# Four small tiles move from behind the tile sets to ahead of them in SBUF

## The chip, the cores and the metric

The kernel runs on one core of a Trainium2 chip. Its time is device microseconds of one execution. TensorE (PE in the profile) multiplies, VectorE (DVE) and ScalarE (ACT) do arithmetic on tiles, GpSimd (POOL) does some of it too, SyncE (SP) issues the DMAs. Tiles live in SBUF, 128 partitions each with its own run of bytes; matmuls write to PSUM. A matmul has a stationary operand, loaded first by a weight load (PEld), and a moving operand that streams through column by column.

## The reference

Two encoder layers over 512 tokens of width 1024 in float32, each a mixer and an MLP, then a last RMSNorm. Layer 0 mixes with dilated window attention (16 heads in three groups of window and dilation), layer 1 with differential attention (8 heads, two maps each), both with a relative bias table.

```
for i in range(2):
    hn  = rms_norm(h, norm_mix_g[i])
    mix = dilated_window_attention(hn, ...) if i == 0 else differential_attention(hn, ...)
    h   = h + mix
    u   = relu(rms_norm(h, norm_mlp_g[i]) @ w_in[i])      # 1024 -> 4096
    h   = h + (u * u) @ w_out[i]                          # 4096 -> 1024
out = rms_norm(h, norm_final_g)
```

## The kernel before

**Data.** Activations lie transposed: the residual h is eight tiles `h0` to `h7` of 128 features by 512 tokens. Every float32 operand of a large product is split in two parts that TensorE multiplies in its fast format: a rounded tile (`Ah`, `Bh`, `Ch`, `whi`) and the remainder (`Al`, `Bl`, `Cl`, `wlo`). `mm3` (line 168) makes one product of three matmuls, lines 169 to 171: rounded by rounded, the weights' rounded part by the remainder, the weights' remainder by the rounded part. A "product" below is one of these matmuls.

**Tile sets.** Set A (eight `Ah`, eight `Al`, from `xset("A")`) holds the input of the current stage: h times the norm's gain, written by `Norm.feed` (lines 232 and 233). Set B holds hidden tiles of the MLP in even chunks, and in attention the split queries of layer 0, the keys of layer 1 and the head outputs (`oh`, `ol`), all under the tags `Bh0` to `Bl7`. Set C, in a pool of the MLP alone, holds the hidden tiles of odd chunks. Layer 0's and layer 1's attention keep their own tiles in the memory that C has later or had before.

**Stages.** `linear_steps` takes a unit of weights, 8 tiles of 128 rows by 256 columns, and for each of its two column tiles sums 8 tiles of the moving set in one PSUM bank: 24 products for a column tile, 48 for a unit, weights stationary, 512 tokens moving. The MLP runs `m_in` (moving: set A) and `m_out` (moving: B or C) in four chunks in the order in 0, in 1, out 0, in 2, out 1, in 3, out 2, out 3; each chunk is four units, 192 products. Hidden chunks 0 and 2 lie in B, 1 and 3 in C. In `values1` (line 739) and in `m_end` (line 660, the last chunk of layer 1) the roles are turned: the set's tile is stationary, 128 tokens of it, and the weights move, 256 columns.

**Weights.** `fetch` (line 140) loads a unit of 1 MB by one DMA into `raw`, ScalarE rounds it to `whi` (line 158) and VectorE makes `wlo` (line 159), two buffers each, one unit ahead.

**The norm.** `Norm.rstd` (line 252) sums squares on TensorE, VectorE scales them to `ms` (line 257), GpSimd raises them to -1/2 into `rstd` (line 259). Both are tiles of 128 partitions by 4 float32. `Norm.rows` (line 261) turns `rstd` into a row for every partition by matmuls with the identity and keeps it in `rB` (and scaled in `rBs`). This happens four times, as hooks among the first products of a stage.

**Layout.** Pools lie one behind the other in the order in which they are opened (lines 87 to 91): `const`, `hpool` (h, A, B), `rpool` (`ms`, `rstd`, `rB` two buffers each, `rBs` one), `wpool` (`raw`, `whi`, `wlo`, two buffers of 8192 bytes a partition each), `spool` (`nacc` one, `nsq` two). Behind them come the pools that open and close with a stage: for the MLP two tiles `u`, then the tiles of C. A tile of 512 float32 takes 2048 bytes a partition. A tile of 4 float32 takes 32, as sizes are rounded up to a multiple of 32.

**Order.** The tile framework plans the instructions of each engine from their dependencies, a model of times and the order in the program, and places the semaphores. It knows a buffer by its tag and the count of its buffers.

Of the kernel before, what the change touches and what calls it, by code (L numbers as in the profile page):

```python
# [11 lines left out]
F32 = mybir.dt.float32  # L12
# [7 lines left out]
P = 128  # L20
# [4 lines left out]
NB = SEQ // P  # L25
# [56 lines left out]
def tile_encoder(ctx: ExitStack, tc: tile.TileContext, x, rel_bias, gains, norm_final_g,  # L82
# [4 lines left out]
    const = ctx.enter_context(tc.tile_pool(name="const", bufs=1))  # L87
    hpool = ctx.enter_context(tc.tile_pool(name="hpool", bufs=1))
    rpool = ctx.enter_context(tc.tile_pool(name="rpool", bufs=2))
# [14 lines left out]
    def t_tile():  # L104
        return ps_t.tile([P, 512], F32, tag="t", name="t_ps")
# [114 lines left out]
    class Norm:  # L220
# [31 lines left out]
        def rstd(self):  # L252
            ps = t_tile()
            for t in range(NB):
                nc.tensor.matmul(ps[:, t:t + 1], self.acc[:, t * P:(t + 1) * P], ones, start=True, stop=True)
            ms = rpool.tile([P, NB], F32, tag="ms", name="ms")
            nc.vector.tensor_scalar(ms, ps[:, 0:NB], 1.0 / DM, EPS, op0=ALU.mult, op1=ALU.add)
            self.r = rpool.tile([P, NB], F32, tag="rstd", name="rstd")
            nc.gpsimd.tensor_tensor(self.r, ms, mhalf[:, 0:NB], op=ALU.pow)

        def rows(self, scaled=None):
# [685 lines left out]
```

## Time and profile before

| | |
|---|---|
| median of three runs | 1250.77 us (1249.84 to 1252.31) |
| profiled execution | 1250.46 us, span 1248.7 us |
| mean granted TensorE clock | 0.993 of full speed |
| PE busy | 98% of the span, 6096 matmuls |
| DVE, ACT, POOL busy | 51%, 40%, 9% |
| DMA | 115.73 MB, 93 GB/s in the mean |

A duration of a matmul in the profile is a latency: matmuls are pipelined, and one begins before the one ahead of it has ended. The pace is the time from start to start; it is read from a stretch whose first and last start are known, divided by the count in it. A share of busy time is a mean over stages.

### The profile page before, as it was taken

The page shows a single profiled execution, that of the slowest core. Times are in us where ns is not written, and L with a number is a line of the kernel's source. Part 1 is how long each engine was busy: PE and PEld are TensorE (multiplying, and loading weights), DVE is VectorE, ACT ScalarE, POOL GpSimd, SP SyncE. Part 2 cuts the span into 40 slices and gives each one's busy share as a digit, 9 for nine tenths or more (in the row PEclk, how much of TensorE's full clock was granted, in tenths as well). Part 3 has the DMA queues.
Part 4 walks back from the last instruction along what each step waited for, and adds up shares of the span by engine and source line. Part 5 has one row for each costly group of instructions (what it writes and reads, how often), then busy time and mean ns, then how long its engine had stood idle before and what let it go on. Part 6 is the DMA issues. An engine that isn't in the chain of part 4 may idle for free.

```text
span 1248.7 us, 15250 instructions
## 1 busy us (share of the span) xinstructions
PE 1223.2 (98%) x6096; PEld 1019.1 (82%) x6096; DVE 637.8 (51%) x1039; ACT 499.5 (40%) x905; POOL 116.9 (9%) x219
## 2 busy tenths in 40 slices
PE   7989999999999999999999999998999999999997
PEld 5778878788888888888888998987888888888897
DVE  7764455644433434434568677664744334344323
ACT  5452333533422323312357666653534223123133
POOL 5000000200000000000101222312300000000011
PEclk9999999999999999999999999998999999999999
DMA  7261222233223333223422343121333223332211
GB/s 228 67 136 39 68 68 68 68 101 102 97 76 98 101 101 101 75 95 102 145 75 91 98 124 101 65 82 51 101 102 102 85 85 101 101 101 97 75 65 69
DMA packets 108307, 115.73 MB, mean 93 GB/s; under 512 B 4507, under 2 KB 101915, under 8 KB 108187
## 3 DMA queue, kind: packets, MB, share of 16 engines
q1 hardware_dynamic: 108236, 114.75, 29.4%
q8 instruction: 48, 0.79, 0.3%
q14 instruction: 23, 0.19, 0.0%
HBM read 112.50 MB, written 2.24 MB: 92 GB/s over the span
## 4 chain that ended last, share of the span: by engine, by line
PE 95%; DMA 2%; DVE 1%; ACT 1%; POOL 0%; issue 0%; SPq 0%; POOLq 0%; DVEq 0%; ACTq 0%
PE acc L169 15%; PE acc L171 15%; PE acc L170 15%; PE s_ps L170 13%; PE s_ps L171 13%; PE s_ps L169 13%; PE o_ps L800 2%; PE s_ps L345 1%; PE s_ps L346 1%; PE t_ps L791 1%; DMA B<-fd 1%; PE o_ps L525 1%; PE s_ps L494 1%; PE o_ps L529 1%; PE t_ps L485 0%; DMA h<-in_x_dram 0%
## 5 line engine op out<-in xcount | busy, mean ns | idle before, releaser
L158 ACT CAST whi<-raw 128x1024 fp32r<-128x1024 f32 (+1 forms) x194 | 192.6, 1039 | 406.2 <-PE s_ps L170 223.9
L159 DVE TENSOR_TENSOR wlo<-raw,whi 128x1024 fp32r<-128x1024 f32 (+1 forms) x194 | 233.7, 1241 | 23.2 <-ACT whi L158 22.6
L169 PE MATMUL acc<-Ah,whi 128*128 128x512 f32 x472 | 187.8, 398 | 0.0
L171 PE MATMUL acc<-Ah,wlo 128*128 128x512 f32 x472 | 187.7, 398 | 0.0
L170 PE MATMUL acc<-Al,whi 128*128 128x512 f32 x472 | 187.7, 398 | 0.0
L169 PE MATMUL s_ps<-Ah,whi 128*128 128x512 f32 x360 | 143.0, 398 | 6.0 <-ACT whi L158 6.0
L170 PE MATMUL s_ps<-Al,whi 128*128 128x512 f32 x360 | 143.7, 399 | 2.5 <-DVE Al L233 2.4
L171 PE MATMUL s_ps<-Ah,wlo 128*128 128x512 f32 x360 | 142.9, 397 | 0.0
L169 PEld LDWEIGHTS acc<-Ah,whi 128*128 128x128 f32 x472 | 89.0, 188 | 20.6 <-ACT sp L338 0.5
L171 PEld LDWEIGHTS acc<-Ah,wlo 128*128 128x128 f32 x472 | 88.8, 188 | 20.7 <-DVE wlo L159 0.5
L170 PEld LDWEIGHTS acc<-Al,whi 128*128 128x128 f32 x472 | 89.0, 188 | 20.2 <-issue 0.5
L169 PEld LDWEIGHTS s_ps<-Ah,whi 128*128 128x128 f32 x360 | 68.2, 190 | 22.0 <-ACT whi L158 6.0
L170 PEld LDWEIGHTS s_ps<-Al,whi 128*128 128x128 f32 x360 | 68.2, 189 | 20.5 <-DVE Al L233 4.6
L171 PEld LDWEIGHTS s_ps<-Ah,wlo 128*128 128x128 f32 x360 | 68.2, 190 | 16.1 <-DVE wlo L159 0.2
L644 ACT ACTIVATE u<-u 128x512 f32<-128x512 f32 x64 | 40.2, 630 | 101.1 <-DVE u L643 101.1
L653 DVE TENSOR_TENSOR h<-h,s_ps 128x512 f32<-128x512 f32 x33 | 22.7, 687 | 108.5 <-PE s_ps L171 108.5
L250 POOL TENSOR_TENSOR nacc<-nacc,nsq 128x512 f32<-128x512 f32 x18 | 27.5, 1530 | 535.7 <-ACT nsq L248 535.2
L643 DVE SCALAR_TENSOR_TENSOR u<-s_ps,rB 128x512 f32<-128x512 f32 x40 | 27.5, 690 | 89.6 <-PE s_ps L171 82.6
L169 PE MATMUL s_ps<-Bh,whi 128*128 128x512 f32 x152 | 60.0, 395 | 0.0
L170 PE MATMUL s_ps<-Bl,whi 128*128 128x512 f32 x152 | 60.0, 395 | 0.0
L171 PE MATMUL s_ps<-Bh,wlo 128*128 128x512 f32 x152 | 60.0, 395 | 0.0
L775 DVE CUSTOM_DVE_ANT_0 p<-s_ps,bias 128x512 f32<-128x512 f32 x64 | 43.4, 688 | 31.6 <-PE s_ps L346 21.1
(237 smaller groups left out, 2268.7 us busy)
## 6 DMA issues: line engine op xcount, KB each, us to landing
raw<-in_mlp_w_in_dram SPq DMA_DIRECT2D x32, 1024.0 KB, 5.3
raw<-in_mlp_w_out_dram SPq DMA_DIRECT2D x32, 1024.0 KB, 5.2
raw<-in_b_w_qkv_dram SPq DMA_DIRECT2D x12, 1024.0 KB, 5.1
raw<-in_a_w_qkv_dram SPq DMA_DIRECT2D x11, 1024.0 KB, 5.1
bias<-fd SPq DMA_DIRECT2D x16, 448.0 KB, 3.6
raw<-in_a_w_o_dram SPq DMA_DIRECT2D x4, 1024.0 KB, 5.3
raw<-in_b_w_o_dram SPq DMA_DIRECT2D x4, 1024.0 KB, 5.2
h<-in_x_dram SPq DMA_DIRECT2D x8, 256.0 KB, 4.9
```

The lines of the kernel that those rows point to most:

```text
L158: nc.scalar.copy(hi[:, k, c], raw[:, k, c])
L159: nc.vector.tensor_sub(lo[:, k, c], raw[:, k, c], f32(hi[:, k, c]))
L169: nc.tensor.matmul(ps, ahi, bhi, start=first, stop=False)
L170: nc.tensor.matmul(ps, ahi, blo, start=False, stop=False)
L171: nc.tensor.matmul(ps, alo, bhi, start=False, stop=last)
L250: eng.tensor_add(self.acc, self.acc, sq)
L345: nc.tensor.matmul(S, q[m][:, qs], k[m][:, ks], start=True, stop=False)
L643: nc.vector.scalar_tensor_tensor(u, ps, 0.0, nm.rB, op0=ALU.max, op1=ALU.mult)
L644: nc.scalar.activation(u, u, AF.Square)
L653: nc.vector.tensor_add(hT[ct], hT[ct], ps)
L775: nc.vector.tensor_tensor_reduce(out=xt, in0=S, in1=bias[h][m][:, b * P:b * P + SEQ], scale=1.0, scalar=3.0e38, op0=ALU.add, op1=ALU.min, ...
L800: marks["PV"] = nc.tensor.matmul(O[:, b, :], aT[:, k, :], v[:, k, es], start=k == 0, stop=k == NB - 1)
```

## The change

`ms` and `rstd` are taken from the pool `const` instead of `rpool`, again with two buffers each. `const` is opened ahead of `hpool`, so the four tiles, 128 bytes a partition in all, now lie ahead of h and the sets A and B, which move up by 128 bytes; `rB` and everything behind it stays where it was. No instruction is added, removed or given other operands than these tiles.

```diff
@@ -253,9 +253,9 @@
             ps = t_tile()
             for t in range(NB):
                 nc.tensor.matmul(ps[:, t:t + 1], self.acc[:, t * P:(t + 1) * P], ones, start=True, stop=True)
-            ms = rpool.tile([P, NB], F32, tag="ms", name="ms")
+            ms = const.tile([P, NB], F32, tag="ms", name="ms", bufs=2)
             nc.vector.tensor_scalar(ms, ps[:, 0:NB], 1.0 / DM, EPS, op0=ALU.mult, op1=ALU.add)
-            self.r = rpool.tile([P, NB], F32, tag="rstd", name="rstd")
+            self.r = const.tile([P, NB], F32, tag="rstd", name="rstd", bufs=2)
             nc.gpsimd.tensor_tensor(self.r, ms, mhalf[:, 0:NB], op=ALU.pow)
 
         def rows(self, scaled=None):
```

## Rows read from the trace of the kernel before

**Rows 1.** The page of the whole kernel: its head, the busy times of part 1, and of part 4 (the chain that ended last) the shares by engine.
```profile
span 1248.7 us, 15250 instructions
PE 1223.2 (98%) x6096; PEld 1019.1 (82%) x6096; DVE 637.8 (51%) x1039; ACT 499.5 (40%) x905; POOL 116.9 (9%) x219
...
PE 95%; DMA 2%; DVE 1%; ACT 1%; POOL 0%; issue 0%; SPq 0%; POOLq 0%; DVEq 0%; ACTq 0%
```

**Rows 2.** Groups of instructions by line with shapes kept apart, whole kernel: the matmuls of 512 columns, of the three lines 169 to 171 the first alone (the other two have the same counts). Columns: line, engine, operation, out<-in by the program's names, shapes, xcount | busy us, mean ns of one | idle time of the engine before them. `oh` are tiles of set B, `k` are keys in tiles of set B.
```profile
L169 PE MATMUL acc<-Ah,whi 128*128 128x512 f32 x472 | 187.8, 398 | 0.0
...
L169 PE MATMUL s_ps<-Ah,whi 128*128 128x512 f32 x360 | 143.0, 398 | 6.0 <-ACT whi L158 6.0
...
L169 PE MATMUL s_ps<-Bh,whi 128*128 128x512 f32 x152 | 60.0, 395 | 0.0
...
L169 PE MATMUL s_ps<-Ch,whi 128*128 128x512 f32 x112 | 43.6, 389 | 0.0
...
L169 PE MATMUL acc<-Bh,whi 128*128 128x512 f32 x104 | 41.1, 395 | 0.0
...
L169 PE MATMUL acc<-Ch,whi 128*128 128x512 f32 x80 | 31.1, 389 | 0.0
...
L169 PE MATMUL acc<-oh,whi 128*128 128x512 f32 x76 | 30.4, 401 | 0.0
...
L345 PE MATMUL s_ps<-k,qh 128*128 128x512 f32 x64 | 26.7, 417 | 0.0
...
L346 PE MATMUL s_ps<-k,ql 128*128 128x512 f32 x64 | 25.6, 399 | 0.0
...
L169 PE MATMUL s_ps<-oh,whi 128*128 128x512 f32 x52 | 20.5, 398 | 0.0
```

**Rows 3.** Busy time in stretches of the first MLP (the first seven) and the second (the last six); each begins and ends with the start of the first product of a stage. Columns: from:to in us, length, then busy us (xinstructions that touch the stretch) of TensorE's matmuls, its weight loads, VectorE, ScalarE and GpSimd, the granted clock, the DMA share, GB/s. The moving tiles are, in order: A (chunks 0 and 1 of `m_in`), B (`m_out` 0), A (`m_in` 2), C (`m_out` 1), A (`m_in` 3), B (`m_out` 2), C (`m_out` 3); then A (chunks 0 and 1), B, A, C, A, B.
```profile
272.73:347.25 74.52, 74.52 (x322) 59.96 (x321) 34.07 (x42) 30.61 (x44) 0.00 (x0) 1.00 0.31 99
347.25:392.05 44.80, 44.80 (x193) 36.04 (x192) 15.53 (x17) 9.17 (x11) 0.00 (x0) 1.00 0.30 94
392.05:436.85 44.80, 44.80 (x193) 36.04 (x192) 19.53 (x23) 16.49 (x23) 0.00 (x0) 1.00 0.29 94
436.85:480.40 43.55, 43.55 (x194) 36.04 (x192) 15.54 (x17) 9.17 (x11) 0.00 (x0) 1.00 0.30 97
480.40:525.19 44.79, 44.79 (x194) 36.03 (x192) 19.53 (x23) 16.48 (x23) 0.00 (x0) 1.00 0.29 94
525.19:569.99 44.80, 44.80 (x194) 36.04 (x192) 15.54 (x17) 9.16 (x11) 0.00 (x0) 1.00 0.28 94
569.99:613.52 43.53, 43.53 (x193) 36.05 (x192) 23.03 (x23) 16.42 (x23) 7.84 (x6) 1.00 0.30 97
897.52:970.10 72.58, 72.58 (x315) 58.86 (x314) 34.09 (x42) 30.24 (x44) 0.00 (x0) 1.00 0.28 91
970.10:1014.71 44.61, 44.61 (x193) 36.17 (x192) 15.54 (x17) 9.14 (x11) 0.00 (x0) 1.00 0.30 95
1014.71:1059.34 44.63, 44.63 (x194) 36.17 (x193) 19.54 (x23) 16.48 (x23) 0.00 (x0) 1.00 0.29 94
1059.34:1102.88 43.54, 43.54 (x194) 36.03 (x192) 15.55 (x17) 9.17 (x11) 0.00 (x0) 1.00 0.30 97
1102.88:1147.67 44.79, 44.79 (x194) 36.04 (x192) 19.53 (x23) 16.49 (x23) 0.00 (x0) 1.00 0.29 94
1147.67:1192.47 44.80, 44.80 (x193) 35.99 (x192) 15.54 (x17) 9.16 (x11) 0.00 (x0) 1.00 0.28 94
```

**Rows 4.** The same view, columns as before, of two stretches in which the set is loaded as weights and `whi` and `wlo` move, 256 columns: 96 products of `values1` with set A, and 72 of `m_end` with set C.
```profile
637.68:649.07 11.39, 11.39 (x98) 11.39 (x96) 7.68 (x10) 5.35 (x9) 0.00 (x0) 1.00 0.29 94
1196.21:1204.85 8.64, 8.64 (x75) 8.64 (x73) 1.26 (x3) 1.53 (x6) 2.21 (x3) 1.00 0.37 121
```

**Rows 5.** The same view of two longer stretches: the first layer up to the end of its attention heads, and the second layer's attention up to its projection.
```profile
0.00:205.00 205.00, 192.22 (x1010) 157.03 (x1011) 124.31 (x290) 87.84 (x212) 19.70 (x22) 0.98 0.36 98
...
618.00:860.00 242.00, 236.30 (x1418) 208.01 (x1417) 166.92 (x341) 146.06 (x324) 55.28 (x160) 0.99 0.29 92
```

**Rows 6.** Groups by line with shapes kept apart, columns as in rows 2 with what ended the idle time: the rounding of the weights on ScalarE, and the rounding (line 645) and the remainder (line 646) of the MLP's hidden tiles into sets B and C.
```profile
L158 ACT CAST whi<-raw 128x1024 fp32r<-128x1024 f32 x190 | 190.1, 1048 | 405.1 <-PE s_ps L170 223.9 <-PE acc L170 159.1 <-issue 17.1
...
L646 DVE TENSOR_TENSOR Cl<-u,Ch 128x512 fp32r<-128x512 f32 x32 | 22.0, 687 | 21.6 <-ACT Ch L645 21.6
...
L646 DVE TENSOR_TENSOR Bl<-u,Bh 128x512 fp32r<-128x512 f32 x32 | 21.8, 688 | 20.2 <-ACT Bh L645 20.2
...
L645 ACT CAST Ch<-u 128x512 fp32r<-128x512 f32 x32 | 19.9, 621 | 1.0
...
L645 ACT CAST Bh<-u 128x512 fp32r<-128x512 f32 x32 | 19.5, 619 | 0.8
```

**Rows 7.** TensorE's waits in the whole kernel: who waited for whom, us in total, times, longest us.
```profile
PE s_ps L169 <- ACT whi L158: 6.0, 1, 6.0
...
PE s_ps L170 <- DVE Al L233: 2.4, 1, 2.4
```

**Rows 8.** The view of one line, for lines 257 and 259: xcount, duration in ns (min/median/max), first and last start in us, forms.
```profile
L257 DVE TENSOR_SCALAR ms<-t_ps x4: 161/162/163, 32.4 to 891.0; 128x4 f32<-128x4 f32 x4
...
L259 POOL TENSOR_TENSOR rstd<-ms,mhalf x4: 1017/1025/1030, 32.6 to 891.2; 128x4 f32<-128x4 f32 x4
```

## The prediction

> **What bounds the kernel now.** I read the page first. TensorE is busy for 98% of the span and makes up 95% of the chain that ended last [rows 1]. So only what changes the pace of its matmuls, or takes a wait from it, moves the time; nothing else in the change is large. Almost all of that chain is lines 169 to 171, the three products of the split matmul.
>
> Next I read the groups of instructions with shapes kept apart [rows 2]. The same product of 512 columns has a mean of 398 ns when the moving tile is in set A, 395 ns in set B and 389 ns in set C. These are latencies of pipelined instructions, so I looked for the pace: stretches between the first product of one stage and the first of the next, in which TensorE does nothing but 192 products (4 units x 2 column tiles x 8 tiles x 3) [rows 3]. In the first MLP it takes 44.80 us for 192 with B, 44.80 with A, then 43.55 with C, then 44.79 with A again and 44.80 with B, and 43.53 with C. Divided by 192: 233.3 ns a product with A or B, 226.8 with C. The granted clock is 1.00 in all of them, the upper of its two levels, and there are 192 weight loads in each. The stretch with B at 347.25 and the one with C at 436.85 are the same stage (`m_out`) with the same work beside it: VectorE 15.53 and 15.54 us, ScalarE 9.17 and 9.17 us. What differs is the tile that is read. So TensorE loses 6.5 ns on every long product whose moving tile is in A or B, on the path that sets the end.
>
> **Where the tiles lie.** The pools lie one behind the other in the order in which they are opened, so distances follow from tile sizes. From the first tile of A to the first of C there are the 32 tiles of A and B, the four small tiles (32 bytes each, 128 together), three tiles of `rB` and `rBs`, six of 8192 bytes for the weights, three of `nacc` and `nsq`, two of `u`: 131,200 bytes, which is 64 x 2048 + 128. From A to `whi` it is 43 x 2048 + 128. Every tile of A, B and the residual has a length of 2048. So today C and the weights lie at one offset within 2048 bytes, and A, B and h at another, 128 bytes lower; the four small tiles are all that makes the difference. With the change they lie ahead of h, `rB` and everything behind it stays where it was, and A, B and h come to the offset at which C and the weights lie now. (C to A is then exactly 131,072 bytes.)
>
> **The change part by part.** *Instructions:* none is added or removed. The two tags keep two buffers each, so no wait for a buffer is added. VectorE's mean square (162 ns) and GpSimd's power (1025 ns) [rows 8] run four times as before. If the program's order came out otherwise around them and the products that cover them were gone, that would be 4 x 1.2 = 4.7 us; today no wait of TensorE on them is in the list, whose entries of this kind are the first weights, 6.0 us, and one `Al`, 2.4 us [rows 7]. I take 0.
>
> *Long products in the two MLPs.* The reading that I take: the pace follows the offset of the moving tile against the weights (or in itself; both give the same here), so A and B go to 226.8 ns. In the first MLP: 74.52 us for 319 products (321 weight loads less two at the edges) with A, and four stretches of 192: 1087 products x 6.5 = 7.1 us. In the second the paces are 72.58 / 312 = 232.6, then 44.61 and 44.63 / 192 = 232.4, then 44.79 and 44.80 / 192 = 233.3; against 43.54 / 192 = 226.8: 312 x 5.8 + 384 x 5.6 + 384 x 6.5 = 6.5 us [rows 3]. Nothing else is late there: the rounding of the weights on ScalarE waits over 380 us for TensorE to give buffers back [rows 6], so the supply has room, and the stretches with C show that it follows at 226.8. This term is 13.6 us, whole on the path.
>
> *Long products elsewhere.* The counts in [rows 2], three lines each, are 472 + 360 with A, 152 + 104 with B, 76 + 52 with `oh` and `ol` (tiles of B under another name), and 64 + 64 of logits with keys in B: 2496 + 768 + 384 + 128 = 3776. Less 1087 and 1080 this leaves 1609 in attention and the projections. At the smaller difference, 5.6 ns, they hold 9.0 us at most. TensorE is busy for 192.2 of 205 us in the first of these parts and 236.3 of 242 in the second [rows 5], so most of it is on the path, but there the long products stand in short groups between transposes and other products, and some end in a wait. I take three quarters, 6.7 us; the ends are 0 and 9.0.
>
> *Products with A as the weights.* In `values1` the roles are turned: A is loaded and `whi` moves. 96 products of 256 columns take 11.39 us, 118.6 ns each; with C in that place 72 take 8.64 us, 120.0 ns [rows 4]. With A at C's offset 384 of them cost 384 x 1.4 = 0.5 us more. This row also says that A isn't simply a slow place: as weights it is the faster one.
>
> *The other engines.* VectorE's subtraction into B takes 688 ns and into C 687, ScalarE's rounding 619 and 621 [rows 6]: the offset shows in neither. The instructions that read or write h I cost at 0, between -2 and +2 ns each by the same rows; they lie beside TensorE's work.
>
> Sum: -13.6 - 6.7 + 0.5 = -19.8 us. The profiled execution took 1250.46 us (span 1248.7 and 1.8 around it), 0.3 us under the median of the three runs, 1250.77, so it stands for them. 1250.5 - 19.8 = 1230.7; I forecast **1230.5 us**.
>
> [...] [Rows 3] show two paces at one clock and one width, 233.3 and 226.8 ns. [...]
>
> **The rivals.**
> *No change, 1250.5 us.* C is fast for another reason: because it lies above the weights, or in another part of the memory, and not for its offset; or the pools get padded so that nothing moves by 128. For it: the rows show names, not addresses, and C is the only set up there. Against it: the turned roles in [rows 4], where A has the shorter pace, and that everything which could tell A and B from C within 2048 bytes vanishes with the change. [...]
> *Only the clean stretches gain, 1237 us.* The faster pace needs an undisturbed stream. Then the 1609 products elsewhere give 0 and the sum is -13.6 + 0.5 = -13.1. For it: in the second MLP A's pace differs (232.4 against 233.3) before and after the first stage with C, so the pace depends on what went before. Against it: at 436.85 C has its pace from the start of its stretch.
> *Slower, 1275 us.* An equal offset is what collides, with the weights that ScalarE and VectorE write beside each product, and C escapes it by lying above the weight pool. Then A and B lose what they now save: 3776 x 6.5 = 24.5 us more, from the first long product on. It decides only if position and not offset explains C. Against it: the stretch with C at 436.85 has 17 VectorE and 11 ScalarE instructions beside it, the weights' among them, at an equal offset and the best pace of all [rows 3].
>
> **How the numbers follow.** The forecast 0.68, the clean stretches alone 0.19, no change 0.09, slower 0.04. A measurement of this kernel can tell about 0.2% (2.5 us) from no change. Both of the first two are faster by over that: 0.87 faster, 0.09 same, 0.04 slower. The low end: all 9.0 us of the second term and no loss in `values1` give 1227.9, and about 2 us for what the paces leave open, 1226. The high end takes in the clean stretches alone with 2 us of the same: 1239. Left out are no change and slower, and some of the edges.
>
> **What would show it.** Products with A and B at a mean near 389 ns instead of 398 and 395; every stretch of 192 at about 43.5 us whatever the set; `values1` at 11.5 us for 96; the subtractions into A and B, the counts and the waits as they are. The forecast is wrong if the stretch of `m_out` with B still takes 44.8 us; the second term is wrong if only the MLPs become shorter; the sign is wrong if A and B go above 234 ns a product.

## The result and the profile after

The changed kernel takes 1233.35 us (median of four runs, 1232.53 to 1234.28) against 1251.37 us of the kernel before (median of four runs: the three of the table above and one beside the changed kernel): a ratio of 0.9857 with a 95% interval of 0.9845 to 0.987, 18.0 us less. The profiled execution took 1232.82 us. The order of the instructions on each engine is the same in both kernels, and their number too. The page of the changed kernel, against [rows 1]:

```profile
span 1231.0 us, 15250 instructions
...
PE 1206.0 (98%) x6096; PEld 1020.2 (83%) x6096; DVE 637.5 (52%) x1039; ACT 499.3 (41%) x905; POOL 116.3 (9%) x219
...
PE 94%; DVE 2%; DMA 2%; ACT 1%; POOL 0%; issue 0%; SPq 0%; POOLq 0%; DVEq 0%; ACTq 0%
```

The span is 17.7 us shorter, TensorE's busy time 17.2 us. No other engine's busy time moved by more than 0.6 us. The groups with shapes kept apart, columns as in [rows 2]:

```profile
L169 PE MATMUL acc<-Ah,whi 128*128 128x512 f32 x472 | 185.8, 394 | 0.0
...
L169 PE MATMUL s_ps<-Ah,whi 128*128 128x512 f32 x360 | 141.6, 394 | 5.7 <-ACT whi L158 5.5
...
L169 PE MATMUL s_ps<-Bh,whi 128*128 128x512 f32 x152 | 59.2, 389 | 0.0
...
L169 PE MATMUL s_ps<-Ch,whi 128*128 128x512 f32 x112 | 43.6, 389 | 0.0
```

B is at C's 389 ns. A, at 394, is 4 ns lower and not at the 389 that the forecast named; its mean holds the attention too. The stretches of the MLPs, columns as in [rows 3] (A in chunks 0 and 1, B, A, C in the first MLP; A in chunks 0 and 1, B and a later A in the second). The two long ones, here and in [rows 3], begin with the first product behind the norm's matmuls, inside chunk 0, and not with the first of their stage:

```profile
270.57:342.99 72.42, 72.42 (x322) 59.97 (x321) 34.06 (x42) 30.59 (x44) 0.00 (x0) 1.00 0.32 102
342.99:386.51 43.52, 43.52 (x193) 36.04 (x192) 15.55 (x17) 9.18 (x11) 0.00 (x0) 1.00 0.30 97
386.51:430.03 43.52, 43.52 (x193) 36.04 (x192) 19.55 (x23) 16.48 (x23) 0.00 (x0) 1.00 0.30 97
430.03:473.55 43.52, 43.52 (x193) 36.04 (x192) 15.55 (x17) 9.17 (x11) 0.00 (x0) 1.00 0.31 97
886.28:957.12 70.84, 70.84 (x315) 58.66 (x314) 34.11 (x42) 30.25 (x44) 0.00 (x0) 1.00 0.29 95
957.12:1000.64 43.52, 43.52 (x193) 36.04 (x192) 15.55 (x17) 9.18 (x11) 0.00 (x0) 1.00 0.31 97
1087.68:1131.20 43.52, 43.52 (x193) 36.04 (x192) 19.55 (x23) 16.49 (x23) 0.00 (x0) 1.00 0.30 97
```

Every stretch of 192 takes 43.52 us, 226.7 ns a product, whichever set is read. The three sets can no longer be told apart by their pace, and the work of VectorE and ScalarE beside it, its counts and the granted clock are what they were.

### The profile page after: what moved, and what is told of

Same layout as the page of the kernel before. It is cut to its first block, busy times and chain, and to the rows that moved or that the text cites. A ratio compares the mean times of both kernels' runs of the same rounds, so it can differ in the third digit from the quotient of the medians.

```text
span 1231.0 us, 15250 instructions
## 1 busy us (share of the span) xinstructions
PE 1206.0 (98%) x6096; PEld 1020.2 (83%) x6096; DVE 637.5 (52%) x1039; ACT 499.3 (41%) x905; POOL 116.3 (9%) x219
## 4 chain that ended last, share of the span: by engine, by line
PE 94%; DVE 2%; DMA 2%; ACT 1%; POOL 0%; issue 0%; SPq 0%; POOLq 0%; DVEq 0%; ACTq 0%
PE acc L169 15%; PE acc L171 15%; PE acc L170 15%; PE s_ps L170 13%; PE s_ps L171 13%; PE s_ps L169 13%; PE o_ps L800 2%; PE s_ps L345 1%; PE s_ps L346 1%; PE t_ps L791 1%; DMA B<-fd 1%; PE o_ps L525 1%; PE s_ps L494 1%; PE o_ps L529 1%; PE t_ps L485 0%; DMA h<-in_x_dram 0%
```

## The experiments

Three theories stood against each other. *Distance:* the pace follows the offset between a product's moving tile and the weights. *Own address:* it follows the moving tile's offset alone. *Place:* C was fast for where it lies. All kernels compute the whole reference. In what follows an offset is a tile's first byte within 2048 bytes: before, A, B and h had 992, the weights and C 1120; in the changed kernel all have 1120.

**Moving the weights instead.** The small tiles go behind the weights, so that these come down to A and B, and C is left alone:

```diff
-            ms = rpool.tile([P, NB], F32, tag="ms", name="ms")
+            ms = spool.tile([P, NB], F32, tag="ms", name="ms")
...
-            self.r = rpool.tile([P, NB], F32, tag="rstd", name="rstd")
+            self.r = spool.tile([P, NB], F32, tag="rstd", name="rstd")
```

> The four small tiles lie behind the weights: h, A and B are where they were before (offset 992 within 2048 bytes), rB, the weights and nacc come down by 128 to the same 992, C stays at 1120. Theory of the distance (the pace of a long product follows the offset between its moving tile and the weights): A and B now agree with the weights and run at 226.8 ns, C has the 128 bytes and falls to 233 ns; 576 products x 6.5 = 3.7 us over the changed kernel, about 1237 us; a stretch of 192 with C takes 44.8 us, with A or B 43.5. Theory of the own address: A and B at 992 stay at 233, C at 1120 stays at 226.8, about 1251 us as before. Theory of the place (C is fast for where it lies): as before, 1251 us.

Measured: 1237.69 us, 0.9891 of before (0.9875 to 0.9908). Stretches of this kernel with B, A and C, columns as in [rows 3]:

```profile
344.46:387.98 43.52, 43.52 (x193) 36.05 (x192) 15.55 (x17) 9.17 (x11) 0.00 (x0) 1.00 0.31 97
387.98:431.50 43.52, 43.52 (x193) 36.05 (x192) 19.55 (x23) 16.48 (x23) 0.00 (x0) 1.00 0.29 97
431.50:476.30 44.80, 44.80 (x194) 36.04 (x193) 15.57 (x17) 9.15 (x11) 0.00 (x0) 1.00 0.30 94
```

A and B have not moved by a byte against the kernel before and are now fast; C has not moved either and is now slow. The gain of 13.3 us came from moving the weights, with `raw`, `rB`, `nacc` and `nsq` beside them, by 128 bytes. Own address and place both fall with these three rows.

**Moving everything.** 128 unused bytes ahead of h, on top of the change:

```diff
+    const.tile([P, 32], F32, name="pad")
     hT = [hpool.tile([P, SEQ], F32, tag=f"h{d}", name=f"h{d}") for d in range(KT)]
```

> The changed kernel with 128 unused bytes ahead of everything: h, A, B, the weights and C all lie at 1248 within 2048 bytes, all distances as in the changed kernel. Distance: 1233 us, every stretch of 192 at 43.5 us. Own address, if it counts within 256 bytes: A, B and C are all where A and B were before within 256 bytes, all at 233 ns, about 1255 us. Own address within 2048 bytes: unknown, any of 1233 to 1260 us.

Measured: 1233.22 us, 0.9858 (0.9843 to 0.9873). Stretches with B and with C:

```profile
343.25:386.77 43.52, 43.52 (x194) 36.05 (x193) 15.54 (x17) 9.18 (x11) 0.00 (x0) 1.00 0.30 97
430.29:473.81 43.52, 43.52 (x194) 36.05 (x193) 15.54 (x17) 9.17 (x11) 0.00 (x0) 1.00 0.31 97
```

128 bytes more on every offset change nothing as long as the distances are kept.

**How much distance counts.** On top of the change, unused bytes behind B move `rB`, the weights, `nacc` and C together. The edit, for 128 bytes:

```diff
+    rpool.tile([P, 32], F32, tag="pad", name="pad", bufs=1)
     hT = [hpool.tile([P, SEQ], F32, tag=f"h{d}", name=f"h{d}") for d in range(KT)]
```

> The changed kernel with 128 unused bytes behind B: h, A and B stay at 1120, rB, the weights, nacc and C lie 128 higher at 1248. Distance: the weights are again 128 bytes above A and B, as in the kernel before: A and B at 233, C at 226.8, about 1251 us. Own address of A and B: 1233 us for these; C at 1248 could lose 3.7 us, 1237 us.

> As the run before with 64 bytes instead of 128: weights and C at 1184, A and B at 1120. Distance: if what counts is whether the two agree within 64 bytes or less, 1233 us; if within more than 64, A and B lose a part or all, 1240 to 1251 us. Own address of A and B: 1233 us, C open.

> The changed kernel with 32 unused bytes behind B: weights and C at 1152, A, B and h at 1120. Distance, if any difference counts: A and B at 233 as with 64 and 128 bytes, 1251 to 1254 us. If differences under 64 bytes are free: 1233 us. C agrees with the weights and stays at 226.8 either way.

> The changed kernel with 256 unused bytes behind B. Distance counted within 256 bytes: 0 again, 1233 us. Counted within more than 256: A and B at 233, 1251 us. The weights' own tiles lie 512 bytes apart in a unit (two column tiles in a row of 1024), and both have run at the fast pace, so 512 can't be the least that counts if it is more than 256: a pace between, or a split by column tile, would tell against counting within a fixed length.

> The changed kernel with 512 unused bytes behind B. The two column tiles of a unit lie 512 bytes apart and both run at the fast pace in the changed kernel, so distances of 512 and 1536 are already in it beside 0 and 1024: the theory of the distance says 1233 us, every stretch of 192 at 43.5 us. At 1251 us the distance between tiles' first bytes would matter and not that of the column tile that is loaded.

> The changed kernel with 224 unused bytes behind B, 32 short of the 256 that gave the fast pace. Distance counted within 256 bytes, any remainder slow: A and B at 233, C at 226.8, 1249 to 1254 us. If a remainder counts only on one side (the weights less than 192 bytes further on): 1233 us.

Measured, with the length of a stretch of 192 in which TensorE reads A or B:

| weights above A and B by | time, us | ratio to before (95%) | 192 products |
|---|---|---|---|
| 0 (the change) | 1233.35 | 0.9857 (0.9845 to 0.987) | 43.52 us |
| 32 | 1251.58 | 1.0007 (0.9998 to 1.0016) | 44.80 |
| 64 | 1253.71 | 1.0018 (1.0009 to 1.0028) | 44.80 |
| 128 | 1250.91 | 0.9999 (0.999 to 1.0009) | 44.79 |
| 224 | 1252.76 | 1.0015 (1.0005 to 1.0025) | 44.80 |
| 256 | 1232.93 | 0.9851 (0.9834 to 0.9867) | 43.52 |
| 512 | 1233.27 | 0.9856 (0.9842 to 0.9871) | 43.52 |

Three of the rows behind the table, a stretch with B each, columns as in [rows 3]: at 32 bytes, at 224 and at 256.

```profile
347.53:392.33 44.80, 44.80 (x194) 36.07 (x192) 15.56 (x17) 9.14 (x11) 0.00 (x0) 1.00 0.29 94
```

```profile
349.92:394.72 44.80, 44.80 (x193) 36.02 (x192) 15.55 (x17) 9.16 (x11) 0.00 (x0) 1.00 0.30 94
```

```profile
344.33:387.85 43.52, 43.52 (x193) 36.04 (x192) 15.55 (x17) 9.17 (x11) 0.00 (x0) 1.00 0.31 97
```

At 128 bytes, C and then A in the stage after:

```profile
437.21:480.75 43.54, 43.54 (x193) 36.04 (x192) 15.55 (x17) 9.17 (x11) 0.00 (x0) 1.00 0.30 97
480.75:525.54 44.79, 44.79 (x193) 36.03 (x192) 19.54 (x23) 16.48 (x23) 0.00 (x0) 1.00 0.29 94
```

So among the distances tried it is the remainder by 256 that decides: 0 is fast, 32, 64, 128 and 224 all cost the same 1.28 us in 192 products, but for some stretches at 128 bytes that cost 1.1 (told of at the end). C, which kept its distance to the weights in all of these, stayed at 43.5 to 43.6 us. I had left open for 64 bytes whether it would cost a part; it costs all.

**wlo alone.** 128 unused bytes between `whi` and `wlo`, on top of the change:

```diff
+        if not wpads:
+            wpads.append(wpool.tile([P, 32], F32, tag="pad", name="pad", bufs=1))
         lo = wpool.tile([P, kt, ncol], F32R, tag="wlo", name="wlo")
```

A and B agree with `whi` and not with `wlo`; C agrees with `wlo` and not with `whi`. The edit moves lines 169 to 171 of the products to 171 to 173.

> The changed kernel with 128 unused bytes between whi and wlo: A, B and whi agree at 1120, wlo, nacc and C lie at 1248. Of the three products that share a moving tile two have whi as weights and one wlo. Distance, counted product by product against the one load that runs beside it: with A and B one product of three falls to 233, 3648 / 3 x 6.3 = 7.7 us, with C (which agrees with wlo now and not with whi) two of three, 384 x 6.5 = 2.5 us; 1243 to 1244 us, and which line is slow tells whether a product's own weights count or the next ones. If any disagreement in the stream makes all of it slow: 1251 to 1256 us. If only whi counts: A and B 226.8, C 233, 1237 us.

Measured: 1249.13 us, 0.998 (0.997 to 0.9989), between the two answers I had written down. The timeline of TensorE's matmuls and weight loads in a stretch with B; columns start us, us, engine, line, operation, out<-in:

```profile
360.21 0.39 PE L171 MATMUL s_ps<-Bh,whi 128*128 128x512 f32 x1
360.21 0.19 PEld L172 LDWEIGHTS s_ps<-Bl,whi 128*128 128x128 f32 x1
360.43 0.40 PE L172 MATMUL s_ps<-Bl,whi 128*128 128x512 f32 x1
360.44 0.19 PEld L173 LDWEIGHTS s_ps<-Bh,wlo 128*128 128x128 f32 x1
360.67 0.40 PE L173 MATMUL s_ps<-Bh,wlo 128*128 128x512 f32 x1
360.67 0.19 PEld L171 LDWEIGHTS s_ps<-Bh,whi 128*128 128x128 f32 x1
360.90 0.39 PE L171 MATMUL s_ps<-Bh,whi 128*128 128x512 f32 x1
```

Each weight load begins with a matmul and brings the weights of the next one. From start to start the product of line 171 takes 0.22 us, that of line 172 0.24 and that of line 173 0.23, at this resolution. By the starts in nanoseconds that the trace holds, the means over the stretch's 64 products of each line are 226.7, 232.7 and 234.0 ns: one line is fast and two are slow. Over the stretch it is 44.38 us for 192, 231.1 ns each. With C in the same kernel all three are slow (233.0, 231.9 and 234.9 ns). The stretch with B, then the one with C:

```profile
347.03:391.41 44.38, 44.38 (x194) 36.30 (x192) 15.56 (x17) 9.19 (x11) 0.00 (x0) 1.00 0.29 95
435.78:480.57 44.79, 44.79 (x194) 36.06 (x192) 15.56 (x17) 9.17 (x11) 0.00 (x0) 1.00 0.29 94
```

Both rows fit one count: a product is slow when the weights that are loaded beside it disagree with its moving tile, or when the weights that it uses do. With B that holds for two of three (line 172 has the load of `wlo` beside it, line 173 uses `wlo`): two at 233.3 and one at 226.7 give 231.1, as measured. With C it holds for all three. I had expected one product of three for B and two for C, from the load beside alone; that was wrong. The count was made after the run and has no run of its own. The times also speak against a collision of VectorE's and ScalarE's writes to the weights with the reading: they are busy for 15.6 and 9.2 of 44.4 us, and the slow products go by line, two of every three through the whole stretch.

**h apart.** 128 unused bytes between h and A on top of the change, so that h alone disagrees:

```diff
     hT = [hpool.tile([P, SEQ], F32, tag=f"h{d}", name=f"h{d}") for d in range(KT)]
...
+    hpool.tile([P, 32], F32, tag="pad", name="pad")
```

> The changed kernel with 128 unused bytes between h and A: h alone lies 128 bytes off, A, B, the weights and C agree at 1248. Distance of moving tile and weights: h takes no part, 1233 us, every stretch of 192 at 43.5 us. If h's move was part of the gain: up to 1251 us; what lies between would be h's share.

Measured: 1232.97 us, 0.9857 (0.9842 to 0.9873). A stretch with B:

```profile
345.07:388.59 43.52, 43.52 (x193) 36.04 (x192) 15.55 (x17) 9.17 (x11) 0.00 (x0) 1.00 0.31 97
```

The residual's place takes no part, though VectorE, ScalarE, GpSimd and, in the last stage, TensorE's transposes read it.

**A apart.** The same tile between A and B: A disagrees with the weights, B and C agree.

```diff
     norm = Norm(G_MIX0, "A")
+    hpool.tile([P, 32], F32, tag="pad", name="pad")
```

> The changed kernel with 128 unused bytes between A and B: A is 128 bytes off the weights, B and C agree with them. Distance: stretches of 192 with A 44.6 to 44.8 us, with B and C 43.5; of the gain of 18 us what belongs to B, its other names and the keys is left, 4.9 by its 768 products and 1.5 to 2 by the rest, 6 to 7 us: about 1244 to 1245 us. If the gain needs all the sets to agree with each other: 1251 us.

Measured: 1246.1 us, 0.9961 (0.9946 to 0.9976). Stretches with B, A and C:

```profile
346.38:389.95 43.57, 43.57 (x193) 36.04 (x192) 15.55 (x17) 9.17 (x11) 0.00 (x0) 1.00 0.30 97
389.95:434.74 44.79, 44.79 (x193) 36.04 (x192) 19.55 (x23) 16.46 (x23) 0.00 (x0) 1.00 0.30 94
434.74:478.28 43.54, 43.54 (x194) 36.03 (x192) 15.55 (x17) 9.18 (x11) 0.00 (x0) 1.00 0.31 97
```

Each set follows its own distance, stage by stage. 5.1 us of the gain are left, against 6 to 7 expected. In the profiled run, at 1244.65 us the fastest of the five, B's 768 products give 4.8 us by their starts (44.80 to 43.57 in the first stretch, 1.23 us) and `oh` and `ol` 1.5, both as expected; what takes some of it back lies outside these products, and where it does so in the slower runs is not shown.

No kernel was found that beats the changed one: 256 bytes, 512 bytes, everything up and h apart are within the spread of its runs.

## Why the prediction was right, and where it was not

*The bound and the pace.* Right, and nearly the whole of the result. (Lines 169 to 171 are 84% of the span in the chain of the kernel before, so "almost all" said a little too much.) The difference between B and C in two equal stages [rows 3] was a matter of the distance to the weights; the run that moved the weights and left A, B and C where they were shows it.

*Where the tiles lie.* Right: the four small tiles were all that kept A and B apart from C and the weights. That the agreement would have to hold within 256 bytes (43.52 us for 192 at 256, 44.80 at 224) I didn't know; the change makes the distances whole multiples of 2048, so it held in any case.

*Long products in the MLPs, -13.6 us.* Right to the tenth. First MLP: 74.52 - 72.42, three times 44.80 - 43.52 and 44.79 - 43.52 make 7.2 us (forecast 7.1). Second: 72.58 - 70.84, 44.61 - 43.52, 44.63 - 43.52, 44.79 - 43.52 and 44.80 - 43.52 make 6.5 us (forecast 6.5). Together 13.7 of the 17.7 us.

*Long products elsewhere, -6.7 us.* The mechanism was right and this term was mis-sized. What is left for it is 17.7 - 13.7 + 0.4 (the next term as measured) = 4.4 us, two thirds of the forecast. Two attention parts between the same instructions, before and after; columns as in [rows 3]:

```profile
31.38:202.05 170.67, 166.44 (x907) 137.71 (x905) 98.12 (x261) 67.19 (x185) 1.44 (x5) 0.99 0.30 75
649.07:840.09 191.02, 191.02 (x1151) 167.91 (x1150) 142.37 (x303) 124.97 (x284) 46.35 (x135) 1.00 0.29 93
```

```profile
31.16:200.92 169.76, 165.04 (x907) 138.01 (x906) 98.19 (x260) 67.08 (x185) 1.44 (x5) 0.98 0.31 76
639.26:828.93 189.67, 189.67 (x1151) 168.04 (x1150) 142.35 (x303) 124.78 (x283) 46.43 (x135) 1.00 0.29 93
```

They became 0.9 and 1.35 us shorter. In the first TensorE works 1.4 us less, and its idle time goes from 4.23 to 4.72 us: a third of what the products gave went into one wait for VectorE, before and after:

```profile
PE s_ps L345 <- DVE mnN L451: 4.2, 1, 4.2
```

```profile
PE s_ps L345 <- DVE mnN L451: 4.7, 1, 4.7
```

In the second it is busy throughout, and the products gain less than in a long stream.

The 4.4 us are a net. By the starts of all 6096 matmuls, which come in the same order in both traces, the 1609 products with the waits between them take 4.9 us less, 3.1 ns each, against the 4.2 ns each of the forecast. (137 of them stand in chunk 0 of the two MLPs, ahead of the long stretches, not in attention.) The first product of the kernel starts 0.5 us earlier. About 1.1 us goes the other way in short products that the forecast left out: behind two of TensorE's waits for VectorE, the one on `mnN` and one of 5.2 us on line 845, the granted clock is at the lower of its two levels, 0.50, and in this trace that reaches further into the work that follows: to 74.8 and 842.8 us, 4.2 and 6.0 us behind the ends of the waits, against 3.4 and 4.5 us in the trace of the kernel before. (With 0.1 us in C's stretches these make the 4.4.) From the first to the last of eight products of line 800 behind the second wait, before and after, columns as in [rows 3]:

```profile
852.28:853.22 0.94, 0.94 (x8) 0.94 (x8) 0.06 (x2) 0.85 (x3) 0.56 (x2) 0.92 0.00 0
```

```profile
841.12:842.77 1.65, 1.65 (x8) 1.65 (x8) 0.70 (x5) 1.28 (x3) 0.56 (x2) 0.50 0.00 0
```

The alignment doesn't decide this: the 256 products of line 800 take 28.8 us by their starts, without a wait among them, in the changed kernel and 28.0 in the one before, but also 28.0 with 256 bytes and with h apart, where the distances have the same remainders as in the changed kernel.

I had argued from the share of busy time that three quarters would stay on the path; a share of 94% says that TensorE waits little, not that a short group of products between transposes reaches the pace of a long one. The forecast named this as a rival (the clean stretches alone, 1237 us); the truth lies between the two, nearer to the forecast.

*Products with A as the weights, +0.5 us.* Right. The 96 products of the first `values1`, against 11.39 us in [rows 4]:

```profile
627.75:639.26 11.51, 11.51 (x97) 11.51 (x96) 7.83 (x11) 5.51 (x9) 0.00 (x0) 1.00 0.29 93
```

0.12 us for 96 make 0.5 us for 384 if the four are alike; by their starts all 384 take 0.4 us more.

*The other engines, 0.* Right. The subtraction into B takes 689 ns and into C 689, and the sums into h 688 against 687 before. The same line, after:

```profile
L646 DVE TENSOR_TENSOR Bl<-u,Bh 128x512 fp32r<-128x512 f32 x32 | 21.8, 689 | 20.2 <-ACT Bh L645 20.1
```

*Nothing new to wait for.* Right: TensorE's waits of [rows 7] are 5.5 and 1.7 us now, no new one has come into the list for the norms, and the order is the same.

```profile
PE s_ps L169 <- ACT whi L158: 5.5, 1, 5.5
...
PE s_ps L170 <- DVE Al L233: 1.7, 1, 1.7
```

*The rivals.* "No change" rested on C's place; the run with the weights moved down contradicts it: C, where it was, took 44.80 us for 192 there, and A and B, where they were, 43.52. "Slower", by a collision at an equal offset, had the sign wrong: equal offsets are the fast case at all of 0, 256 and 512 bytes, 43.52 us for 192 in each. By the count above the load beside a product shows in its pace: with `wlo` alone moved, line 172 takes 232.7 ns with the load of `wlo` beside it and line 171, with the same weights in use and a load of `whi` beside it, 226.7. No stretch of 192 took less than 43.52 us, 226.7 ns a product. What in the chip makes the address count, the runs don't show.

The sum was 1230.7 us against 1232.8 in the profiled run: the 2.1 us are the second term, 2.3 us too high, less 0.1 each by which the first and the third came out better.

## What to carry to other kernels

Where the matmul stream is the bound, compare the pace (start to start over a counted stretch) of equal products that read different buffers; a difference of 3% between stages with equal work (44.80 against 43.55 us) was the sign of the layout here. It was enough that the moving tiles and the weights begin at the same remainder by 256 bytes (1233.35, 1232.93 and 1233.27 us with 0, 256 and 512 between, 1250.9 to 1253.7 with 32, 64, 128 and 224); small tiles of 32 bytes in a pool between large ones shift everything behind them, so put them ahead of all the large pools, or pad. In this kernel the gain was whole where the stream is long, and less than half of it per product in short groups (4.9 us in 1609, 3.1 ns each with their waits, against 6.5).

## What was not expected

The cost isn't graded: at 32, 64, 128 and 224 bytes alike a stretch of 192 products takes 44.80 us instead of 43.52, which is 233.3 ns a product of 512 columns instead of 226.7. A single product doesn't take this mean: by the starts, at 128 bytes products take 229 and 238 ns in turn, at 64 bytes 231 and 236. (The shorter stretches at 128 bytes are told of below.)

Products of 256 columns with the set as weights go the other way: 118.6 ns when they disagree by 128 bytes [rows 4], 119.9 (11.51 us for 96) when they agree. Here the difference is graded: the same 96 take 11.20 us at 32 bytes, 11.30 at 64, 11.40 at 128 and 11.36 at 224. C does the same: its 72 products of [rows 4], 8.64 us there, take 8.55 in the kernel with the weights moved down, where C is the one that disagrees. The rows at 32 bytes and of C:

```profile
638.00:649.20 11.20, 11.20 (x97) 11.20 (x96) 7.69 (x10) 5.35 (x9) 0.00 (x0) 1.00 0.28 95
```

```profile
1184.29:1192.84 8.55, 8.55 (x75) 8.55 (x73) 1.26 (x3) 1.53 (x6) 2.20 (x3) 1.00 0.37 123
```

The alignment that helps the one form here, by 6.6 ns a product of 512 columns, costs the other a little, 1.3 ns one of 256.

In the kernel before, at 128 bytes, the second MLP runs at 232.4 ns until its first stage with C and at 233.3 after [rows 3]. In the kernel with the weights 128 bytes up the first MLP begins so too; its first stretch with B:

```profile
347.98:392.59 44.61, 44.61 (x194) 36.17 (x193) 15.55 (x17) 9.16 (x11) 0.00 (x0) 1.00 0.30 94
```

The starts in these shorter stretches follow a pattern that repeats after seven products, from 228 to 241 ns. At 64 bytes the second MLP has the slower of the two paces there as well:

```profile
971.73:1016.53 44.80, 44.80 (x193) 36.10 (x192) 15.56 (x17) 9.15 (x11) 0.00 (x0) 1.00 0.29 95
```

That makes 0.7 of the 2.7 us by which the kernel with 64 bytes is slower than the one before (72.87 against 72.58 us, 44.80 against 44.61 and 44.63); where the rest lies is not shown. Why the stream keeps one of two paces for a whole stage at the one distance and not at the other stays open.
